# Layer B's x operands by token tile, its token sums taken in layer A's output projection, and its head norms' squares on ScalarE

## The chip, the cores and the metric

The kernel runs on one core of one Trainium2 chip. The metric is the device time of one execution in microseconds. A core has five engines with queues of their own: TensorE (PE; its weight loads are shown as PEld), VectorE (DVE), ScalarE (ACT), GpSimd (POOL) and SyncE (SP), which here issues the DMAs. Each engine works through its instructions in the order of the program and waits on semaphores for what others produce.

## The reference

Two attention layers run over 2048 prompt tokens and 64 sample tokens, `D_MODEL` = 1024, heads of 64, in float32. What is computed, cut to what matters here:

```python
def rms_norm(x, g):
    return x * rsqrt(mean(x * x, -1) + EPS) * g

def layer(x, norm_g, w_in, q_g, k_g, w_out, ...):
    h = rms_norm(x, norm_g)                      # one scale per token
    q, k, v, gate = split(h @ w_in)
    q, k = rms_norm(q, q_g), rms_norm(k, k_g)    # one scale per token and head
    o = softmax(q k^T / 8 + bias) v              # over a band of chunks of 64 tokens
    return x + (o * silu(gate)) @ w_out
```

Layer A has 16 query heads over 2 key heads and a window of 3 chunks, layer B has 16 heads with keys of their own and a window of 9 chunks. The kernel also returns the newest keys and values of both layers (for layer B the last 512 prompt tokens and the sample's).

## The kernel before

**Numbers as two parts.** A float32 product is made of three float32r products: x is split into `xh` (ScalarE's cast) and `xl` (GpSimd's subtraction x - xh), the weights into `wh` (ScalarE, times the norm's gain) and `wl` (VectorE), and PE adds `xh wh + xh wl + xl wh` (lines 481 to 483 in `project`). The sample's 64 tokens take two products, with the parts of x side by side in one stationary operand (474 to 477).

**Order of the work.** The tokens are cut into units of 256 (two tiles of 128), `u` = 0 to 7, and the sample, `u` = 8, which goes before unit 7. PE's order is written out by hand: `layer_a` and `layer_b` each have an attention pipeline, and in between its steps a `Filler` feeds the projections as jobs: layer A's input projections (four quarters `qd` of heads over all units), layer A's output projection (two halves of the outputs, eight jobs `j` of `OT` = 264 tokens each), layer B's input projections (eight head pairs `hp` over all units), layer B's output projection. When a job starts, `Filler.step` (622) runs the splits of its x and prefetches the x of the job after it; the weights of the third job ahead start with `WN - 8` = 5 pieces (640). The pipelines run the jobs as far as marks (`filler.to`, `PACE_B`) say. The instructions of the other engines are put in order by a planner that simulates the times; small tasks wait in the queue `bg` (`Background`) and are let in by `share` and `drain`, urgent ones first.

**x of layer B.** `load_act` (351) loads four pieces of a unit, each 256 inputs by all tokens of the unit, into `xraw`, a ring of `XB` = 3 buffers, and splits them into the ring `xx` of `XN` = 7 (lines 385, 386). For head pair 0 the split parts are also stored to `xsb` in DRAM (389); the other pairs load them from there (362). Each `xx` buffer is used by both token tiles of the unit, since a tile's projection runs over all eight blocks of 128 inputs.

**Token scales.** For layer B, `load_act` squares each piece on ScalarE into `res` (397) and adds it on VectorE into `sqr` (401, 403). `token_scales` (423) lets PE sum over the partitions with `ones` (430), VectorE takes mean and epsilon (`ms`, 433), and GpSimd the power of -1/2 (`rms`, 437). In layer B it is called in the first pair, after the first tile's products of each unit, with a result buffer of the ring `pj` of two, which the projections also use. In layer A, units 0 and 1 do likewise; for the others `row_scales` (444) loads the rows of x once more, four halves a unit, into the same ring `xraw` (454), and ScalarE squares and sums them (456).

**Behind a projection.** `evacuate` (490) empties `pj` on ScalarE with the token's scale (503). `head_norm` (511) takes each head's sum of squares on VectorE, one instruction a head (521), GpSimd the power (525), and VectorE scales (530). `gate` uses ScalarE's Tanh (538) into the ring `sq` of two, and `store_kv` (548) multiplies keys on GpSimd into `ko`, a single buffer (551), and stores them (552).

**Output projection.** `output_jobs` (1248) loads two blocks of the residual x into `res` (1275), PE makes 24 products for each of four blocks `m` of 128 outputs (1280 to 1282), VectorE adds (1285), and every second block is stored to `x1` (layer A) or `y` (1287).

Of the kernel before, what the change touches and what calls it, by code (L numbers as in the profile page):

```python
# [33 lines left out]
XB = 3  # L34
XN = 7
EARLY = 3
MORE = 4.7
WN = 13
# [13 lines left out]
def hybrid_encoder_kernel(  # L52
# [61 lines left out]
    mhalf = const([P, 4], "mhalf")  # L114
# [111 lines left out]
    xs = [dr.tile([P, 2 * KC * TOK], F32, tag=n, name=n) for n in ("xsa", "xsb")]  # L226
# [124 lines left out]
    def load_act(src, o, T, squares=False, joint=False, lead=None, cache=None, cached=False):  # L351
# [14 lines left out]
        def fetch():  # L366
            c = len(raws)
            if c < 4:
                raw = t("xraw", [P, 2 * OT], XB)
                rv = raw[:, : 2 * T].rearrange("p (k s) -> p k s", k=2)  # L370
                held["last"] = load(rv, src[:, 2 * c : 2 * c + 2, o : o + T]).ins
                raws.append(rv)
# [21 lines left out]
        def square(c):  # L394
            def fn():
# [4 lines left out]
                part = t("sqr", [P, 2 * T if joint else T], 2)  # L400
# [20 lines left out]
    rr = [const([P, NT + 1], f"rms{l}") for l in range(2)]  # L421

# [21 lines left out]
    def row_scales(unit):  # L444
# [4 lines left out]
        for i, (_, t0, n) in enumerate(tiles):  # L449
            r0 = (tt + i) * P  # L450
            for h in range(2):
                raw = t("xraw", [P, 2 * OT], XB)
# [11 lines left out]
        nc.gpsimd.tensor_tensor(rr[0][:, tt : tt + w], v[:, :w], mhalf[:, :w], op=ALU.pow)  # L464

# [24 lines left out]
    def evacuate(layer, tt, n, ps, C, G, b=None):  # L490
        a = t("pa", [P, 384], 4)
        pieces = [(a[:, : C - G], ps[:, : C - G])]
        if G:
            out = a
            if b is None:
                b = t("pb", [P, 256], 5)
# [14 lines left out]
    def head_norm(n, src):  # L511
        H = src.shape[1] // HD
        f = []

        def squares():
            sq = t("sq", [P, 256], 2)
            f.append(t("f", [P, 4], 3))
# [14 lines left out]
        return [bg.put(0.15 * H, squares, True), bg.put(0.1 * H, scale, True)]  # L532
# [79 lines left out]
    class Filler:  # L612
# [9 lines left out]
        def step(self):  # L622
            if self.gen is None:
# [13 lines left out]
                if self.n + EARLY < len(self.jobs):  # L637
                    nxt = self.jobs[self.n + EARLY]
                    if nxt.weights is not None and nxt.early:
                        nxt.weights(WN - 8)  # L640
# [17 lines left out]
    def layer_a():  # L658
# [4 lines left out]
        def add_unit(qd, place, unit):  # L663
# [8 lines left out]
            def prefetch():  # L672
# [3 lines left out]
                cache = None if qd < KEEP[u] else xs[0]  # L676
# [308 lines left out]
    def layer_b():  # L985
# [4 lines left out]
        def add_unit(hp, unit):  # L990
# [7 lines left out]
            def prefetch():  # L998
                for j in range(NO):
                    assert finished["x1", j] == 2 or j * OT >= u * UT + T  # L1000
                st.x[hp, u] = x = load_act(x1, u * UT, T, hp == 0, T == TS, None, xs[1], hp > 0)
                return x

            def weights(*m):
                if hp not in st.emit:
                    (st.w[hp],), _, st.emit[hp] = load_weights(1, (w_in_b[hp], 512))
                st.emit[hp](*m)

            def gen():
                xc = st.x.pop((hp, u))  # L1010
                it.prs, it.todo = [], []
                it.gate = t("pb", [P, 2, P], 5)
                for e, (tt, t0, n) in enumerate(tiles):
                    out = []
                    c = yield from project((tt, t0, n), xc, st.w[hp], 512, out)
                    if hp == 0 and e == 0:
                        token_scales(1, unit, xc, psum("pj", 512, 2))
                    pr = evacuate(1, tt, n, out[0], 512, P, it.gate[:, e])
                    it.prs.append(pr)
                    v, kn = pr[:n, 256:384], pr[:n, 128:256]  # L1020
                    split_v(n, v, VS[:, 2] if last else VT[:, tt])
# [400 lines left out]
```

## Time and profile before

| | |
|---|---|
| median of 3 runs | 2317.17 us (2315.77 to 2439.61) |
| profiled execution | 2318.61 us, span 2316.8 us, mean granted clock 0.996 |
| busy, share of the span | PE 98%, PEld 86%, DVE 67%, ACT 62%, POOL 37% |
| DMA | 379.37 MB, mean 164 GB/s |
| layer A's start (0 to 130 us) | PE busy 109.57 us |
| layer A's output projection (690 to 864.7 us) | PE busy 174.41 of 174.70 us |
| layer B's first head pair (864.7 to 1015 us) | PE busy 135.79 of 150.30 us |
| a later head pair (1452.2 to 1606.5 us) | PE busy 153.48 of 154.30 us |

How it is read: the page gives busy time by engine; the windows view gives it for stretches, with the granted clock of TensorE; the waits view says for whom an engine waited (engine, own buffer and line, then the releaser; total us, times, longest us); the lines view groups instructions (count, busy us, mean ns of one, idle before them). Matmuls are pipelined, so their mean durations overlap, and a busy PE need not be at its peak. A wait for several semaphores is put down to the one that came last.

### The profile page before, as it was taken

What the parts mean: (1) busy time and instruction counts of PE and PEld (TensorE: products, weight loads), DVE (VectorE), ACT (ScalarE), POOL (GpSimd) and SP (SyncE); (2) the same over time, 40 slices, a digit from 0 to 9 for tenths busy, and PEclk for the clock granted to TensorE, in tenths of its full rate; (3) what the DMA queues carried; (4) which work ended last, traced back from release to release, by engine and by line L of the source; (5) the groups of instructions that cost most, each with busy time, mean ns of one, the idle gap of its engine ahead of it and who ended that gap; (6) DMA issues with size and microseconds to landing.
All of it is one profiled execution on the core that took longest, in us unless ns stands there. A gap on an engine that the chain in (4) does not pass through costs nothing. (4 is left out here: it accounts for less than half of the span.)

```text
span 2316.8 us, 42427 instructions
## 1 busy us (share of the span) xinstructions
PE 2262.0 (98%) x13981; PEld 1987.5 (86%) x13981; DVE 1548.6 (67%) x5198; ACT 1427.1 (62%) x3628; POOL 855.9 (37%) x1235
## 2 busy tenths in 40 slices
PE   8899999999999999999999999999999999999999
PEld 6787888888889997878888888888888888889999
DVE  7679989888782227776766767767667677676211
ACT  6778877777773326765665666656656666566321
POOL 5554533333255445442222222322322223224443
PEclk9999999999999999999999999999999999999999
DMA  7846546754446766454454543544444435443665
GB/s 252 255 156 204 168 125 204 234 172 148 143 136 200 221 206 232 140 181 150 134 158 128 151 147 105 179 135 138 152 129 151 147 101 179 133 126 107 192 185 147
DMA packets 232126, 379.37 MB, mean 164 GB/s; under 512 B 24721, under 2 KB 163361, under 8 KB 231873
## 3 DMA queue, kind: packets, MB, share of 16 engines
q1 hardware_dynamic: 231904, 376.65, 52.8%
q8 instruction: 110, 1.80, 0.3%
q14 instruction: 112, 0.91, 0.1%
HBM read 296.13 MB, written 82.08 MB: 163 GB/s over the span
## 5 line engine op out<-in xcount | busy, mean ns | idle before, releaser
L481 PE MATMUL pj<-wh,xx 128*128 128x512 f32 (+1 forms) x1648 | 669.6, 406 | 17.1 <-ACT pb L503 7.2
L483 PE MATMUL pj<-wh,xx 128*128 128x512 f32 (+1 forms) x1648 | 639.4, 388 | 0.0
L482 PE MATMUL pj<-wl,xx 128*128 128x512 f32 (+1 forms) x1648 | 636.3, 386 | 0.0
L483 PEld LDWEIGHTS pj<-wh,xx 128*128 128x128 f32 x1648 | 311.3, 189 | 67.4
L481 PEld LDWEIGHTS pj<-wh,xx 128*128 128x128 f32 x1648 | 312.7, 190 | 58.7 <-ACT pb L503 8.4
L386 POOL TENSOR_TENSOR xx<-xraw,xx 128x528 fp32r<-128x528 f32 (+1 forms) x200 | 264.9, 1340 | 223.6 <-ACT xx L385 216.9
L482 PEld LDWEIGHTS pj<-wl,xx 128*128 128x128 f32 x1648 | 313.4, 190 | 37.9
L525 POOL TENSOR_TENSOR f<-f,mhalf 128x4 f32<-128x4 f32 (+3 forms) x221 | 228.1, 1032 | 221.9 <-DVE f L521 212.1
L1118 ACT ACTIVATE p<-p,nm 128x640 f32<-128x640 f32 (+5 forms) x272 | 204.3, 751 | 169.9 <-DVE nm L1114 167.8
L1280 PE MATMUL pj<-xx,wh 128*128 128x264 f32 x1024 | 293.3, 286 | 0.3 <-DVE res L1285 0.3
L1281 PE MATMUL pj<-xx,wh 128*128 128x264 f32 x1024 | 291.3, 284 | 0.0
L1282 PE MATMUL pj<-xx,wl 128*128 128x264 f32 x1024 | 289.8, 283 | 0.0
L1114 DVE CUSTOM_DVE_ANT_0 p<-sb,BT 128x640 f32<-128x640 f32 (+5 forms) x272 | 196.6, 723 | 114.9 <-PE sb L1108 111.5
L567 DVE TENSOR_TENSOR pl<-sb,ph 128x640 fp32r<-128x640 f32 (+5 forms) x272 | 194.5, 715 | 112.4 <-ACT ph L566 109.8
L385 ACT CAST xx<-xraw 128x528 fp32r<-128x528 f32 (+1 forms) x200 | 123.5, 626 | 217.7 <-PE pj L1282 119.2
L981 POOL TENSOR_TENSOR o<-gt,o 128x256 f32<-128x256 f32 (+2 forms) x140 | 107.1, 765 | 372.4 <-issue 150.8
L566 ACT CAST ph<-sb 128x640 fp32r<-128x640 f32 (+5 forms) x272 | 164.4, 604 | 118.9 <-PE sb L594 114.2
L1285 DVE TENSOR_TENSOR res<-pj,res 128x264 f32<-128x264 f32 x128 | 55.0, 431 | 248.3 <-PE pj L1282 237.3
L1280 PEld LDWEIGHTS pj<-xx,wh 128*128 128x128 f32 x1024 | 192.7, 188 | 1.0 <-DVE res L1285 0.5
L1281 PEld LDWEIGHTS pj<-xx,wh 128*128 128x128 f32 x1024 | 192.4, 188 | 0.2
L1282 PEld LDWEIGHTS pj<-xx,wl 128*128 128x128 f32 x1024 | 192.6, 188 | 0.0
L521 DVE CUSTOM_DVE_ANT_0 sq<-pa 128x64 f32<-128x64 f32 (+1 forms) x850 | 169.8, 252 | 23.3 <-ACT pa L503 21.2
(191 smaller groups left out, 4822.8 us busy)
## 6 DMA issues: line engine op xcount, KB each, us to landing
xx<-xsb SPq DMA_DIRECT2D x224, 512.0 KB, 4.3
xx<-xsa SPq DMA_DIRECT2D x88, 512.0 KB, 4.7
xraw<-oga SPq DMA_DIRECT2D x64, 264.0 KB, 3.4
xraw<-ogb SPq DMA_DIRECT2D x64, 264.0 KB, 3.3
xsa<-xx SPq DMA_DIRECT2D x32, 512.0 KB, 4.4
wraw<-in_w_in_b_dram SPq DMA_DIRECT2D x64, 256.0 KB, 3.5
xsb<-xx SPq DMA_DIRECT2D x32, 512.0 KB, 3.7
xraw<-in_x_dram SPq DMA_DIRECT2D x40, 256.0 KB, 4.1
```

Of the source, the lines that this page charges most:

```text
L386: nc.gpsimd.tensor_tensor(xl, rv, xh.bitcast(F32), op=ALU.subtract)
L481: nc.tensor.matmul(ps[:n, :C], xh, wh, start=k == 0, stop=False)
L482: nc.tensor.matmul(ps[:n, :C], xh, wl, start=False, stop=False)
L483: nc.tensor.matmul(ps[:n, :C], xl, wh, start=False, stop=k == KC - 1)
L521: nc.vector.tensor_tensor_reduce(out=sq[:n, c], in0=src[:, c], in1=src[:, c], op0=ALU.mult, op1=ALU.add, scale=1.0, scalar=HD * EPS, accum ...
L525: nc.gpsimd.tensor_tensor(fv, fv, mhalf[:n, :H], op=ALU.pow)
L567: b = nc.vector.tensor_tensor(dst_lo, src, dst_hi.bitcast(F32), op=ALU.subtract)
L1114: mi = nc.vector.tensor_tensor_reduce(out=p[:n, :nk], in0=S[:n, o : o + nk], in1=bias[:n, b0 : b0 + nk], op0=ALU.add, op1=ALU.min, scale=1 ...
L1118: ex = nc.scalar.activation(p[:n, :nk], p[:n, :nk], AF.Exp, scale=-1.0, bias=nmh, accum_out=it.sm[:n, 2 * i + h : 2 * i + h + 1],)
L1280: nc.tensor.matmul(ps[:, :OT], wh, oh, start=k == 0, stop=False)
L1281: nc.tensor.matmul(ps[:, :OT], wh, ol, start=False, stop=False)
L1282: nc.tensor.matmul(ps[:, :OT], wl, oh, start=False, stop=k == KC - 1)
```

## The change

- **x of layer B** is loaded by `load_b` as four operands a unit: one token tile (of two) by half of the inputs (`A11`, `A12` for the first tile, `A21`, `A22` for the second), kept in DRAM as `xo`, one slot an operand; the sample is one operand. `project_b` uses them tile by tile. The loads from `x1` go in runs of 128 tokens.
- **Token sums of layer B** are taken in layer A's output projection: `add_squares` squares the two finished blocks on ScalarE and adds them on VectorE to a sum per token, behind the next block's residual addition. `scales_of` makes the scales for tiles 0 to 11 ahead of unit 0's first products and for the rest ahead of unit 1's. The sums lie in the rings `ev` and `row` and in parts of the bias tile `BT`.
- **Head norms in layer B** use `squares_whole`: one Square on ScalarE for all heads of a tile, one `tensor_reduce` and one `tensor_scalar` on VectorE. Layer A keeps one instruction a head.
- **Buffers**: `xraw` 5 (was 3), weight parts 15 (13) with still 5 early pieces, `pb` 6 (5), `f` wider; `sqr` and `ko` are gone, the partial sums of layer A's first units go to `ev` and `ko` to the ring `sq`. The scratch for software-made DMA descriptors shrinks to 1024.
- The diff also adds `block_weights`, `product`, `gen_blocks`, `gen_sample` and, in `load_b`, `sums`, which form products of sums of blocks. They are used for head pairs from `PLAIN` on; `PLAIN` is 8 and the head pairs are 0 to 7.

```diff
+XR = 5
+PLAIN = 8
+S_FIRST = (6, 7)
-WN = 13
+WN = 15
+WP = 5
...
-    xs = [dr.tile([P, 2 * KC * TOK], F32, tag=n, name=n) for n in ("xsa", "xsb")]
+    xs = dr.tile([P, 2 * KC * TOK], F32, tag="xsa", name="xsa")
+    xo = dr.tile([P, 8 * NU + 1, 8 * P], F32, tag="xo", name="xo")
...
-                raw = t("xraw", [P, 2 * OT], XB)
+                raw = t("xraw", [P, 2 * OT], XR)
...
-                part = t("sqr", [P, 2 * T if joint else T], 2)
+                part = t("ev", [P, 256], 4)[:, : 2 * T if joint else T]
...
+    def add_squares(half, m, o, rv):
+        s2 = t("p", [P, 640], 3)[:, : 2 * OT].rearrange("p (k s) -> p k s", k=2)
+        nc.scalar.activation(s2, rv, AF.Square)
+
+        def fn():
+            if half or m == 3:
+                nc.vector.tensor_tensor(s2[:, 0], s2[:, 0], s2[:, 1], op=ALU.add)
+            cut = (o // UT + 1) * UT
+            for t0, t1 in ((o, cut), (cut, o + OT)):
+                a, b = (s2[:, k, t0 - o : t1 - o] for k in range(2))
+                acc = sums_of(t0, t1 - t0)
+                if half or m == 3:
+                    b = acc
+                nc.vector.tensor_tensor(acc, a, b, op=ALU.add)
...
+        return fn
+
+    def scales_of(t0, t1):
+        ps = psum("o", 512, 1)
+        w = t1 - t0
+        for i in range(w):
+            tok = (t0 + i) * P
+            nc.tensor.matmul(ps[:, 2 * i : 2 * i + 2], sums_of(tok, P), ones, start=True, stop=True)
+        v = t("f", [P, 16], 3)[:, :w]
+        nc.vector.tensor_scalar(
+            v, ps[:, : 2 * w].rearrange("p (i e) -> p i e", e=2)[:, :, 0], 1.0 / D, EPS, op0=ALU.mult, op1=ALU.add
+        )
+        nc.gpsimd.tensor_tensor(rr[1][:, t0:t1], v, mhalf[:, :w], op=ALU.pow)
...
+    def project_b(e, n, xc, w, res):
+        ps = psum("pj", 512, 2)
+        for k in range(KC):
+            wh, wl = weights_of(w, k)
...
+                xh, xl = (a[:, k % 4] for a in xc.op["A%d%d" % (e + 1, k // 4 + 1)])
+                nc.tensor.matmul(ps, xh, wh, start=k == 0, stop=False)
+                nc.tensor.matmul(ps, xh, wl, start=False, stop=False)
+                nc.tensor.matmul(ps, xl, wh, start=False, stop=k == KC - 1)
...
+    def load_b(unit, hp):
...
+        def cached(n, i):
+            xx = t("xx", [P, 4 * OT], XN, F32R)
+            held["last"] = load(xx[:, : 8 * P].bitcast(F32), xo[:, i]).ins
+            return xx
+
+        def split(xx, xh, xl, rv, i):
+            nc.scalar.copy(xh, rv)
+            nc.gpsimd.tensor_tensor(xl, rv, xh.bitcast(F32), op=ALU.subtract)
+            store(xo[:, i], xx[:, : 8 * P].bitcast(F32))
...
+        def raws():
+            for e in range(2):
+                for i in range(2):
+                    r = t("xraw", [P, 2 * OT], XR)[:, :512].rearrange("p (k s) -> p k s", k=4)
+                    held["last"] = load(r, x1[:, 4 * i : 4 * i + 4, u * UT + e * P : u * UT + e * P + P]).ins
+                    raw["A%d%d" % (e + 1, i + 1)] = r
...
+    def head_norm(n, src, whole=False):
...
+        def squares_whole():
+            sq = t("sq", [P, 256], 2)
+            f.append(t("f", [P, 16], 3)[:, :4])
+            fv = f[0][:n, :H]
+            nc.scalar.activation(sq[:n, : H * HD], src, AF.Square)
+            nc.vector.tensor_reduce(fv, sq[:n, : H * HD].rearrange("p (h d) -> p h d", d=HD), axis=AX.X, op=ALU.add)
+            nc.vector.tensor_scalar(fv, fv, HD * EPS, 1.0, op0=ALU.add, op1=ALU.mult)
+            nc.gpsimd.tensor_tensor(fv, fv, mhalf[:n, :H], op=ALU.pow)
...
-            ko = t("ko", [P, 2 * HD], 1)
+            ko = t("sq", [P, 256], 2)[:, : 2 * HD]
...
-                st.x[hp, u] = x = load_act(x1, u * UT, T, hp == 0, T == TS, None, xs[1], hp > 0)
+                st.x[hp, u] = x = load_b(unit, hp)
...
+                if hp == 0 and unit is order[0]:
+                    scales_of(0, 12)
+                if hp == 0 and unit is order[1]:
+                    scales_of(12, NT + 1)
...
-                    c = yield from project((tt, t0, n), xc, st.w[hp], 512, out)
-                    if hp == 0 and e == 0:
-                        token_scales(1, unit, xc, psum("pj", 512, 2))
-                    pr = evacuate(1, tt, n, out[0], 512, P, it.gate[:, e])
...
+                    c = yield from project_b(e, n, xc, st.w[hp], out)
+                    pr = evacuate(1, tt, n, out[0], 512, P, gt[:, e])
...
                     nc.vector.tensor_tensor(rv[:, m % 2], ps[:, :OT], rv[:, m % 2], op=ALU.add)
+                    if "sq" in held:
+                        held.pop("sq")()
                     if m % 2:
                         store(xout[:, c : c + 2, o : o + OT], rv)
+                        if layer == 0:
+                            held["sq"] = add_squares(half, m, o, rv)
+                            if half == 1 and j == NO - 1 and m == 3:
+                                held.pop("sq")()
...
-    nc = _bacc.Bacc("TRN2", target_bir_lowering=False, num_devices=1)
+    nc = _bacc.Bacc("TRN2", target_bir_lowering=False, num_devices=1, dynamic_dma_scratch_size=1024)
```

More of the change, by code (lines that the diff above doesn't have):

```diff
@@ L451, in row_scales @@
             for h in range(2):
[L452 removed]
+                raw = t("xraw", [P, 2 * OT], XR)
                 for d in range(0, P, n):
@@ new lines, in product @@
+    def product(ps, xc, parts, p, start):
+        xh, xl = xc.op[OPERAND[p]]
+        for k in range(4):
+            wh, wl = parts(PIECE[p], k)
+            nc.tensor.matmul(ps[:, :256], xh[:, k], wh, start=start and k == 0, stop=False, skip_group_check=not start)
+            nc.tensor.matmul(ps[:, :256], xh[:, k], wl, start=False, stop=False, skip_group_check=not start)
+            nc.tensor.matmul(ps[:, :256], xl[:, k], wh, start=False, stop=k == 3, skip_group_check=not start)
+            if k < 3:
+                yield 3 * 256 / 2400
@@ L530, in scale @@
             nc.vector.tensor_tensor(sv, sv, fv.unsqueeze(2).to_broadcast([n, H, HD]), op=ALU.mult)
-        return [bg.put(0.15 * H, squares, True), bg.put(0.1 * H, scale, True)]
+        return [bg.put(0.15 * H, squares_whole if whole else squares, True), bg.put(0.1 * H, scale, True)]
     def gate(n, g):
@@ L1005, in weights, with take_qk @@
                 if hp not in st.emit:
-                    (st.w[hp],), _, st.emit[hp] = load_weights(1, (w_in_b[hp], 512))
+                    if hp < PLAIN:
+                        (st.w[hp],), _, st.emit[hp] = load_weights(1, (w_in_b[hp], 512))
+                    else:
+                        st.w[hp], st.emit[hp] = block_weights(w_in_b[hp])
                 st.emit[hp](*m)
+            def take_qk(e, pr):
+                n = tiles[e][2]
+                it.prs[e] = pr
+                it.todo += head_norm(n, pr[:n, 0:256], True)
@@ L1032, in add_unit @@
+            if T < UT:
+                it.cost = 8 * 2 * 512 / 2400
+            else:
+                it.cost = (8 * 6 * 512 if hp < PLAIN else 7 * 12 * 256) / 2400
+            filler.total += it.cost
             it.mark = filler.total
-            filler.add(prefetch, weights if u == 0 else None, gen)
+            filler.add(prefetch, weights if u == 0 else None, gen if hp < PLAIN else gen_blocks if T == UT else gen_sample)
         for hp in range(8):
@@ L1046, in queries @@
             tp = psum("tp", 512, 1)
-            for pr, (tt, t0, n) in zip(it.prs, tiles):
+            for e, (tt, t0, n) in enumerate(tiles):
+                pr = it.prs[e]
                 for j in range(2):
@@ L1210, in pipeline @@
                 if x + 2 < len(its):
+                    if its[x + 2].hp >= PLAIN and len(heads) == 4:
+                        end = c0 + 0.875 * PACE_B * len(heads)
                     near = its[x + 2].mark
```

293 lines of the change are left out of this document (274 added, 19 removed).

## The prediction

> **What bounds the kernel now.** I read the page first.
>
> ```profile
> span 2316.8 us, 42427 instructions
> ## 1 busy us (share of the span) xinstructions
> PE 2262.0 (98%) x13981; PEld 1987.5 (86%) x13981; DVE 1548.6 (67%) x5198; ACT 1427.1 (62%) x3628; POOL 855.9 (37%) x1235
> ```
>
> TensorE (PE) is without work for 2316.8 - 2262.0 = 54.8 us in all. The change takes no matmul away and makes none shorter, so 54.8 us, and what a lowered clock costs on top, is all that it can win. Where is that idle time? The windows view by stage answers (busy time of each engine in each stretch; the columns behind POOL are the granted clock, the DMA share and GB/s):
>
> ```profile
> 0.00:130.00 130.00, 109.57 (x621) 92.45 (x622) 88.69 (x300) 91.84 (x238) 68.54 (x104) 0.97 0.79 245
> 690.00:864.70 174.70, 174.41 (x1426) 173.69 (x1427) 44.21 (x96) 53.68 (x96) 78.41 (x69) 1.00 0.70 206
> 864.70:1015.00 150.30, 135.79 (x728) 113.38 (x727) 119.45 (x359) 102.78 (x249) 80.48 (x90) 0.98 0.57 193
> 1452.20:1606.50 154.30, 153.48 (x907) 132.67 (x905) 108.39 (x369) 97.05 (x245) 43.62 (x72) 1.00 0.47 142
> 108.00:120.00 12.00, 9.47 (x52) 8.03 (x51) 8.15 (x23) 8.67 (x23) 7.87 (x10) 0.86 0.84 272
> 866.00:876.00 10.00, 7.95 (x29) 6.49 (x30) 4.03 (x7) 3.54 (x7) 5.24 (x5) 0.83 0.95 326
> 924.00:936.00 12.00, 10.30 (x49) 8.50 (x48) 8.76 (x34) 6.08 (x17) 5.23 (x7) 0.86 0.23 77
> 1009.00:1021.00 12.00, 8.48 (x44) 7.62 (x44) 8.49 (x27) 5.69 (x13) 3.75 (x6) 0.86 0.58 183
> ```
>
> The first row is layer A's start: 20.4 us idle. The second is layer A's output projection: 0.3 us idle, and VectorE (DVE) busy for only 44 of 175 us. The third is layer B's first head pair, where x is split and squared: 14.5 us idle, the thickest spot behind the start. The fourth is one of the later head pairs: 0.8 us of 154.3. The last four rows are short stretches behind the longest stalls; the clock drops there to 0.83 to 0.86, which costs 0.14 x 12 or 0.17 x 10 = 1.7 us each.
>
> Who ends PE's idle time in 864 to 1015 us (waits view: total, times, longest):
>
> ```profile
> PE pj L481 <- DVE ms L433: 6.1, 5, 3.5
> PE pj L481 <- ACT xx L385: 2.3, 1, 2.3
> PE sb L594 <- DVE nm L1114: 2.1, 3, 1.7
> PE sb L594 <- DVE pl L567: 1.4, 1, 1.4
> PE o L1185 <- DVE pl L567: 1.4, 2, 1.0
> PE sb L594 <- ACT sq L538: 0.7, 1, 0.7
> ```
>
> The first row is `token_scales`: its sums stand in a buffer of the two-deep ring `pj` until VectorE has read them, and the next projection waits for that buffer. In layer A's start (30 to 130 us), PE's longest entry and ScalarE's (ACT) two longest, the latter for 0 to 130 us, are:
>
> ```profile
> PE pj L481 <- ACT pb L503: 7.2, 5, 2.5
> ```
> ```profile
> ACT res L456 <- DMA xraw<-in_x_rows_dram: 17.2, 15, 3.0
> ACT xx L385 <- DMA xraw<-in_x_dram: 7.4, 8, 2.7
> ```
>
> ScalarE empties `pj` late because, in its own order, it stands before that for 17.2 + 7.4 = 24.6 us at loads into `xraw`, a ring of three through which each unit sends eight loads.
>
> **The change, part by part.** With `PLAIN = 8` every head pair (0 to 7) takes the plain path: `block_weights`, `gen_blocks`, `gen_sample` and the `sums` of `load_b` never run. PE gets the same matmuls in the same shapes, the sums' matmuls included. What runs differently is this.
>
> *Token sums.* Out of layer B's first pair go 36 Squares (9 units of 4), 36 + 27 adds, `ms` and its waits:
>
> ```profile
> L397 ACT ACTIVATE res<-xraw 128x512 f32<-128x512 f32 x40 | 25.1, 629 | 8.6 <-DVE sqr L401 5.8 <-DMA xraw<-x 1.8 <-DVE ms L433 0.8
> ```
> ```profile
> L401 DVE TENSOR_TENSOR sqr<-res 128x256 f32<-128x256 f32 x40 | 29.0, 726 | 18.7 <-ACT res L397 11.0 <-PE pj L430 6.8
> ```
>
> They come back as 32 Squares of 528 columns in the output projection (32 x 0.63 = 20 us, ACT from 54 to 74 of 175 us) and 88 adds; at the 0.42 us of L403 below, too much as half are short pieces, 37 us (DVE from 44 to 81 of 175). Those engines have the room: cost 0. If the cover failed, it would be by `res` coming free late behind the Square; the Square runs beside the store of the same tile, so I expect nothing. The new `scales_of` sits ahead of units 0 and 1 in PE's order, its sums are finished a job earlier, and it uses `o`, not `pj`. So the 6.1 us go (bounds 0, if the wait only changes its name, and 6.1).
>
> *`xraw` from three to five.* The 2.3 us stall at the border to layer B, by SyncE's issues and VectorE (timeline: start, length):
>
> ```profile
> 859.79 2.10 SPq L371 DMA_DIRECT2D xraw<-x  x2
> 861.94 0.46 SPq L1287 DMA_DIRECT2D x<-res  x1
> 863.75 0.37 SPq L1275 DMA_DIRECT2D res<-in_x_dram  x1
> ```
> ```profile
> 866.72 0.77 DVE L1285 TENSOR_TENSOR res<-pj,res 128x264 f32<-128x264 f32 x2 [1.21 <-DMA res<-in_x_dram]
> ```
>
> Loads of x for layer B hold SyncE's queue from 859.79 on, because the ring of three is full; the residual load behind them is issued at 863.75 only, and VectorE empties `pj` at 866.72. With five buffers and no Square holding them the loads go at once: the 2.3 us go. In layer A's start a row load now waits for the read three loads before it; with five, only for loads whose data the unit before has already used, so the 24.6 us of ACT should mostly go and of PE's 7.2 us I take 0.8, 5.8 us (bounds 0 and 7.2), with the 1.7 us of clock behind them.
>
> *DVE late in the first pair.* Of the rest (2.1 + 1.4 + 1.4 + 0.7, and 0.2 in a row not shown, 5.8 us) the timeline shows a cause:
>
> ```profile
> 903.17 0.42 DVE L403 TENSOR_TENSOR sqr<-sqr,sqr 128x256 f32<-128x256 f32 x1
> 903.69 1.33 DVE L401 TENSOR_TENSOR sqr<-res 128x256 f32<-128x256 f32 x1
> ```
> ```profile
> 903.37 1.37 POOL L386 TENSOR_TENSOR xx<-xraw,xx 128x512 fp32r<-128x512 f32 x1
> ```
>
> The add at 903.69 takes 1.33 us where the same shape took 0.42 just before: it ends (905.02) 0.3 us behind GpSimd's (POOL) subtraction (904.74). GpSimd's splits stay, the adds that they hold go; I take half, 2.9 us (bounds 0 and 5.8). [...]
>
> *Clock in the first pair.* The dips behind 864.7 and 1010 follow waits that go (2.3 and 3.5 us): 2 x 1.7 = 3.4 us. The dip at 924 to 936 I leave.
>
> *Norm squares in layer B.* Per 128-token tile, four products become one Square, one reduction and one small operation:
>
> ```profile
> L521 DVE CUSTOM_DVE_ANT_0 sq<-pa 128x64 f32<-128x64 f32 x64 | 11.5, 234 | 0.1
> L530 DVE TENSOR_TENSOR pa<-pa,f 128x256 f32<-128x256 f32 x17 | 8.1, 477 | 3.7 <-POOL f L525 3.5
> ```
> ```profile
> L538 ACT ACTIVATE sq<-pb 128x256 f32<-128x256 f32 x64 | 26.8, 418 | 1.2
> ```
> ```profile
> L433 DVE TENSOR_SCALAR ms<-pj x9: 147/154/156, 875.4 to 1013.9; 128x4 f32<-128x4 f32 x8, 128x2 f32<-128x2 f32 x1
> ```
>
> The products cost 11.5 / 16 = 0.72 us a tile (rows of one head pair, 1452 to 1606 us). A reduction over 256 columns is not in the trace; it reads one 256-wide input, so between half and the whole of L530, 0.24 to 0.48, I take 0.42 (L403 above). With 0.15 for the small one: 0.57, so DVE wins 0.15 x 17 = 2.6 us a pair, and ACT gets 17 x 0.42 = 7.1 us (97 to 104 of 154). Neither is the bound. What is late there now:
>
> ```profile
> PE sb L594 <- DVE nm L1114: 3.7, 6, 0.9
> PE o L1185 <- DVE pl L567: 1.2, 5, 0.2
> ```
>
> That is 4.9 us over seven pairs (1015 to 2080 us), where the next pair's weights are split just then. Two more weight buffers (`WN` 15) let two of the three late splits move ahead; the Square on ACT works against it. I take 0 (bounds -4.9 and the second rival).
>
> *Operands by tile and half.* Four loads of 512 KB a unit as before, but the first buffer is free after a quarter of the unit, not after 10 of 16 steps, and the sample's four loads become one. SyncE's longest wait is just this release:
>
> ```profile
> SPq L362 <- PE pj L483: 460.9, 192, 10.5
> ```
>
> PE never waits for these loads in the later pairs (rows above), so the shorter wait buys nothing there. In the first pair x comes in runs of 512 bytes in place of 1 KB; 32 loads, a job ahead of use: 0.
>
> *`ko` moves into the ring `sq`.* New wait: a Square or Tanh two allocations on must wait until the store of `ko` has landed, and ACT's whole queue (exponentials, `ph`, the emptying of `pj`) stands behind it.
>
> ```profile
> out_dram<-ko SPq DMA_DIRECT2D x33, 64.0 KB, 3.5
> ```
> ```profile
> 1464.91 0.46 POOL L551 TENSOR_TENSOR ko<-pa,kgr 128x128 f32<-128x128 f32 x1 [1.09 <-DVE sm L1125]
> ```
> ```profile
> 1469.50 0.31 ACT L538 ACTIVATE sq<-pb 64x128 f32<-64x128 f32 x1
> ```
>
> Product 0.46 and landing 3.5 make 4.0 us; the next user came 4.6 us after it began. So it fits, barely: cost 1 us (bounds 0 and the third rival).
>
> **Sum.** 6.1 + 2.3 + 2.9 = 11.3 and 3.4 of clock in the first pair, 5.8 + 1.7 = 7.5 at the start, less 1: 21.2 us. The profiled execution took 2318.6 us, 1.8 more than its span; 2318.6 - 21.2 = 2297.4. The median of the runs, 2317.17, lies 1.4 under the profiled one: **2296 us**.
>
> **Rivals.** *The waits only change their names* (the next late thing, the splits on ACT and POOL, takes their place): only the 6.1 us go, 2318.6 - 6.1 - 1.4 = 2311. For it: POOL's 80 of 150 us in the first pair stay, and ACT stood at two kinds of load at the start. Against: each wait has its own cause in the rows.
>
> *ScalarE becomes late in layer B.* 136 tiles x 0.42 = 57 us more on ACT; if half of each Square reaches PE, 28.5 us, and the gains stay: 2296 + 29 = 2325. Against: ACT is busy 97 of 154 us, and no wait of the later pairs in the rows above ends on it. [...]
>
> *The store of `ko` holds ScalarE* (slower). 40 stores in layer B (5 a pair, by the code: four tiles and the sample). If the planner puts the next users right behind, each is held up to 4.0 us; if half reaches PE, 40 x 2.0 = 80: 2296 + 80 = 2376. It makes the kernel slower from 21 / 40 = 0.5 us each, and by over 2% (46 us) from 67 / 40 = 1.7 us. For it: the margin of 0.6 us above. Against: the order of ACT is planned with that wait known.
>
> **Chances.** Forecast 0.73, names only 0.14, ScalarE late 0.07, `ko` 0.06. The forecast's own range: all bounds that favour it (6.1 + 2.3 + 5.8 + 5.0 + 7.2 + 1.7 + 4.9 = 33) give 2284, less 2 for stalls not counted, 2282; without the start's 7.5 and half of the DVE part, 2307. With the two middle rivals the range is 2282 to 2324. A change of 2%, 46 us, is about what a measurement of this kernel tells from none. To win that, nearly all of the 54.8 us must go: 0.02, from the forecast's share. Slower by over 2% is `ko`'s case, mostly: 0.05. The rest, 0.93, within.
>
> **What would show it.** Right: no wait on `ms` and none of 2 us at the border to layer B; the first pair's idle under 5 us with at most one clock dip; ScalarE's wait for `in_x_rows` under 8 us; PE's 0.8 us in a later pair unchanged, ACT there at 104 us. Wrong: a wait on `f`, `sq` or `pa` of PE in layer B, ACT idle before Square or Tanh with the store of `sq` as its releaser, or idle time on `res` in the output projection.

## The result, and the profile after

The changed kernel takes **2289.11 us** (median of 5 runs, 2288.97 to 2293.63) against 2317.17 us (5 runs beside it): a ratio of 0.9884, 95% interval 0.9869 to 0.99, so 23 to 30 us faster. Predicted were 2296 us and a range of 2282 to 2324. The page of the changed kernel begins:

```profile
span 2287.3 us, 41688 instructions
## 1 busy us (share of the span) xinstructions
PE 2250.9 (98%) x13981; PEld 1984.5 (87%) x13981; DVE 1539.7 (67%) x4400; ACT 1466.8 (64%) x3757; POOL 854.8 (37%) x1225
```

PE's idle time fell from 54.8 to 36.4 us, and its busy time by 11.1 us with the same 13981 matmuls, so the busy time held losses too, in part a lowered clock (0.996 before, 0.998 after on average). To see where the 29.5 us of span went, both traces are cut at the same matmuls of PE's order. The windows view of the changed kernel at those cuts (columns as in the prediction):

```profile
0.00:119.50 119.50, 107.51 (x622) 92.54 (x623) 91.74 (x306) 94.87 (x249) 72.63 (x108) 0.99 0.86 280
119.50:226.30 106.80, 103.47 (x618) 88.25 (x617) 90.76 (x326) 87.39 (x239) 54.43 (x86) 1.00 0.57 182
677.40:856.20 178.80, 176.34 (x1427) 175.23 (x1427) 94.50 (x172) 69.54 (x124) 83.55 (x70) 0.99 0.69 205
856.20:991.40 135.20, 131.13 (x729) 111.63 (x727) 90.29 (x206) 92.14 (x230) 74.16 (x85) 0.99 0.63 212
1426.50:1579.60 153.10, 152.86 (x905) 132.42 (x905) 103.52 (x266) 102.05 (x263) 43.57 (x72) 1.00 0.48 143
991.40:2047.50 1056.10, 1054.91 (x6240) 913.30 (x6241) 712.55 (x1826) 700.46 (x1804) 298.95 (x495) 1.00 0.48 143
2047.50:2287.30 239.80, 230.91 (x1847) 226.50 (x1845) 78.03 (x170) 81.11 (x163) 99.15 (x94) 1.00 0.51 150
```

| stage (us) | before | after | difference | forecast |
|---|---|---|---|---|
| layer A's start (to 240.0 in before) | 240.0 | 226.3 | -13.7 | -7.5 |
| rest of layer A | 450.0 | 451.1 | +1.1 | 0 |
| layer A's output projection | 174.7 | 178.8 | +4.1 | 0 |
| layer B's first pair | 150.3 | 135.2 | -15.1 | -14.7 |
| the seven later pairs | 1065.0 | 1056.1 | -8.9 | +1 |
| the end, with layer B's output projection | 236.8 | 239.8 | +3.0 | 0 |

The first pair came as forecast, the start gave twice as much, the later pairs gave what was forecast as nothing, and three stages got longer. PE's waits in the first pair and in the two stages that lost most (waits view: first pair; layer A's output projection; the end):

```profile
PE tp L850 <- DVE pa L786: 2.8, 1, 2.8
PE sb L850 <- DVE pl L823: 1.2, 1, 1.2
```
```profile
PE pj L1664 <- DVE res L1669: 2.5, 3, 1.8
```
```profile
PE sb L850 <- DVE nm L1496: 2.1, 1, 2.1
...
PE pj L1664 <- DVE res L1669: 0.9, 1, 0.9
```

The waits on `ms` and the border stall are gone. In their place stand one wait for a head norm (`pa`), waits for residual sums (`res`) and, near the end, one for the softmax (`nm`).

### The profile page after: what moved, and what is told of

Same layout as the page of the kernel before. It is cut to its first block, busy times and chain, and to the rows that moved or that the text cites. A ratio compares the mean times of both kernels' runs of the same rounds, so it can differ in the third digit from the quotient of the medians.

```text
span 2287.3 us, 41688 instructions
## 1 busy us (share of the span) xinstructions
PE 2250.9 (98%) x13981; PEld 1984.5 (87%) x13981; DVE 1539.7 (67%) x4400; ACT 1466.8 (64%) x3757; POOL 854.8 (37%) x1225
## 5 line engine op out<-in xcount | busy, mean ns | idle before, releaser
L529 PE MATMUL pj<-wh,xx 128*128 128x512 f32 x1024 | 421.9, 412 | 0.0
L531 PE MATMUL pj<-wh,xx 128*128 128x512 f32 x1024 | 403.6, 394 | 0.0
L530 PE MATMUL pj<-wl,xx 128*128 128x512 f32 x1024 | 402.8, 393 | 0.0
L391 POOL TENSOR_TENSOR xx<-xraw,xx 128x528 fp32r<-128x528 f32 (+1 forms) x168 | 225.1, 1362 | 196.6 <-ACT xx L390 187.1
L728 PE MATMUL pj<-wh,xx 128*128 128x512 f32 (+1 forms) x624 | 245.5, 393 | 1.7 <-ACT pb L750 1.2
L729 PE MATMUL pj<-wl,xx 128*128 128x512 f32 (+1 forms) x624 | 232.7, 373 | 2.3 <-DVE wl L320 2.3
L730 PE MATMUL pj<-wh,xx 128*128 128x512 f32 (+1 forms) x624 | 233.4, 374 | 0.0
L531 PEld LDWEIGHTS pj<-wh,xx 128*128 128x128 f32 x1024 | 192.6, 188 | 45.1 <-POOL xx L649 0.4
L530 PEld LDWEIGHTS pj<-wl,xx 128*128 128x128 f32 x1024 | 194.1, 190 | 23.1
L529 PEld LDWEIGHTS pj<-wh,xx 128*128 128x128 f32 x1024 | 193.5, 189 | 23.4
L769 POOL TENSOR_TENSOR f<-f,mhalf 128x4 f32<-128x4 f32 (+1 forms) x136 | 137.8, 1013 | 193.6 <-DVE f L768 178.0
```

The lines of the kernel that those rows point to most:

```text
L391: nc.gpsimd.tensor_tensor(xl, rv, xh.bitcast(F32), op=ALU.subtract)
L529: nc.tensor.matmul(ps, xh, wh, start=k == 0, stop=False)
L530: nc.tensor.matmul(ps, xh, wl, start=False, stop=False)
L531: nc.tensor.matmul(ps, xl, wh, start=False, stop=k == KC - 1)
L728: nc.tensor.matmul(ps[:n, :C], xh, wh, start=k == 0, stop=False)
L729: nc.tensor.matmul(ps[:n, :C], xh, wl, start=False, stop=False)
```

## The experiments

Twelve kernels ran. Their profiles, cut at the same matmuls (us; the last column is the median of the runs, for which the kernel before had 2317.12, 2315.59 and 2317.27 in the three sets; `a_oldops`, `a_wn13`, `a_res3` and `a_ko` belong to the second, `a_wn14`, `a_dvesplit`, `a_13n` and `b_xr_sums` to the third). Medians of different sets are compared by their ratios to the kernel before. A stage's time comes from one profiled execution, and a dip of the clock in it weighs: in the changed kernel the granted clock was 0.50 from 702.40 to 705.80 us, and 3.4 us at half the clock are 1.7 us.

| kernel | start | rest of A | output A | first pair | later pairs | end | span | median |
|---|---|---|---|---|---|---|---|---|
| before | 240.0 | 450.0 | 174.7 | 150.3 | 1065.0 | 236.8 | 2316.8 | 2317.17 |
| `b_wn` | 239.2 | 448.7 | 176.3 | 151.6 | 1066.0 | 239.2 | 2321.0 | 2316.51 |
| `b_xr` | 223.8 | 451.2 | 176.7 | 148.1 | 1064.9 | 236.8 | 2301.5 | 2301.58 |
| `b_sums` | 239.2 | 453.0 | 175.8 | 132.3 | 1063.0 | 236.7 | 2300.0 | 2301.44 |
| `b_xr_sums` | 225.0 | 453.2 | 177.3 | 133.0 | 1061.7 | 236.7 | 2286.9 | 2287.88 |
| after | 226.3 | 451.1 | 178.8 | 135.2 | 1056.1 | 239.8 | 2287.3 | 2289.11 |
| `a_oldnorm` | 227.2 | 450.4 | 179.0 | 132.1 | 1058.9 | 240.6 | 2288.2 | 2288.06 |
| `a_oldops` | 226.1 | 449.8 | 176.6 | 137.3 | 1058.8 | 240.5 | 2289.1 | 2291.64 |
| `a_dvesplit` | 225.3 | 449.4 | 178.3 | 130.5 | 1056.5 | 239.4 | 2279.4 | 2283.39 |
| `a_wn14` | 225.5 | 451.2 | 178.8 | 133.3 | 1056.5 | 237.2 | 2282.5 | 2284.1 |
| `a_wn13` | 225.9 | 452.5 | 174.9 | 130.9 | 1056.0 | 236.5 | 2276.7 | 2280.82 |
| `a_res3` | 223.8 | 453.2 | 177.6 | 131.1 | 1057.3 | 236.6 | 2279.6 | 2281.3 |
| `a_ko` | 223.6 | 452.5 | 178.3 | 131.1 | 1056.3 | 236.2 | 2278.0 | 2280.97 |
| `a_13n` | 225.7 | 452.7 | 177.9 | 131.4 | 1058.2 | 237.4 | 2283.3 | 2287.84 |

### `b_xr`: the kernel before, with `xraw` of five

`XR` is 5, at both places that load into `xraw`; the descriptor scratch shrinks as in the change, in all kernels below too.

```diff
-                raw = t("xraw", [P, 2 * OT], XB)
+                raw = t("xraw", [P, 2 * OT], XR)
```

> The kernel before with one part of the change: the ring xraw has five buffers in place of three (and the smaller DMA scratch, which makes the room). Theory: layer A's start was slow because ScalarE stood at loads held back by the ring. Then PE's 7.2 us of waits on the emptying of pj between 30 and 130 us go, ScalarE's wait for in_x_rows falls from 17.2 us to under 8, layer A is some 13 us shorter by the end of its unit loop as in the changed kernel, and the 2.3 us stall at the border to layer B goes; the waits on ms (6.1 us) stay. Time about 2300 us. Rival: the start's gain comes from another part (weight ring, ev ring) or from a new order of the planner; then the start keeps its 7.2 us and the time stays at 2313 to 2317.

Measured: 2301.58 us, ratio 0.9933 (0.9916 to 0.9949). The start shrinks by 16.2 us, more than twice the 7.5 forecast, and the other stages take 0.9 us more together. Of the 16.2 us, 12.5 are idle time of PE (25.6 before, 13.1 here). PE's waits in its first 130 us, and then in its first pair of layer B:

```profile
PE o L482 <- ACT wh L313: 5.8, 1, 5.8
PE o L431 <- DVE sqr L404: 3.0, 1, 3.0
...
PE pj L482 <- DVE ms L434: 5.7, 6, 3.0
PE sb L595 <- DVE nm L1115: 3.3, 4, 1.7
...
PE pj L482 <- ACT xx L386: 1.4, 1, 1.4
```

`PE pj <- ACT pb`, 7.2 us before, is gone altogether. The token sums' waits stay, and of the border stall 1.4 us.

### `b_sums`: the kernel before, with its token sums in layer A's output projection

```diff
-                    if hp == 0 and e == 0:
-                        token_scales(1, unit, xc, psum("pj", 512, 2))
+                if hp == 0 and unit is order[0]:
+                    scales_of(0, 12)
...
+                        if layer == 0:
+                            held["sq"] = add_squares(half, m, o, rv)
```

> The kernel before with layer B's token sums taken in layer A's output projection and no Squares in layer B's first pair; ring of three, x operands and head norms as before. Theory: the 6.1 us of waits on ms go and VectorE's lateness in the first pair falls; the first pair is 8 to 13 us shorter, the border stall of 2.3 us stays or shrinks (no Square holds xraw), and the output projection gets no waits: 2305 us. Rival: the sums make the residual addition late, and the output projection takes 4 to 5 us more as in the changed kernel: 2309 us.

Measured: 2301.44 us, ratio 0.9932 (0.9917 to 0.9946). The first pair falls from 150.3 to 132.3 us. All of PE's waits there:

```profile
PE sb L638 <- ACT sq L582: 0.8, 1, 0.8
PE tp L638 <- ACT pa L547: 0.5, 1, 0.5
```

The ring `xraw` is still three here, and yet the border stall is gone: without the Squares three buffers are enough. In layer A's output projection PE has no wait at all here (175.8 us, 1.1 more than before); but the jobs of that projection begin ahead of the cut, and there PE waits 1.5 us for a residual sum, which it doesn't before, in a stretch that is 3.0 us longer.

### `b_xr_sums`: both together

> The kernel before with the ring xraw of five and the token sums in layer A's output projection; everything else (operands, norms, the ring of weight splits, ko) as before. Theory (these two parts are the whole gain but for the later pairs): 2287 (2285 to 2290), no wait on ms, the first pair as in the changed kernel, later pairs as before at about 154.3 us. Rival (the operands by tile are needed in the first pair, since without them x's loads come late once the sums are gone): 2291 or more, with waits of TensorE on xx or of ScalarE on the loads of x in the first pair.

Measured: 2287.88 us, ratio 0.9873 (0.9854 to 0.9892): 29.4 us, where the two alone gave 15.5 and 15.7. This is all that the whole change gives. The operands, the norms, the ring of weight splits and `ko` together add nothing to it, though the stages are not the same: later pairs 5.6 us shorter in the changed kernel, the other stages 6.0 us longer. The next runs take that balance apart.

### `b_wn`: the kernel before, with 15 buffers for weight splits

```diff
-WN = 13
+WN = 15
-                        nxt.weights(WN - 8)
+                        nxt.weights(5)
```

> The kernel before with 15 weight buffers in place of 13, still 5 pieces early. Theory: the 0.8 us that PE loses at the end of each later head pair comes from the last three pieces of the next pair's weights, which must wait for buffers and are split just then; with two more buffers that wait goes and each later pair takes 1.2 us less, about 7 us in all: 2310 us. Rival: the gain of the later pairs comes from the head norms leaving VectorE; then the later pairs keep their 154.3 us and the time is 2317 within 2.

Measured: 2316.51 us, ratio 0.9999 (0.9988 to 1.0011). Alone, nothing, and the later pairs stay: the rival. (Its profiled execution, 2322.78 us, lay above its median; its stages weigh less.)

### `a_oldnorm` and `a_oldops`: the changed kernel without its norms, and without its operands

```diff
-                it.todo += head_norm(n, pr[:n, 0:256], True)
+                it.todo += head_norm(n, pr[:n, 0:256])
```
```diff
-                st.x[hp, u] = x = load_b(unit, hp)
+                st.x[hp, u] = x = load_act(x1, u * UT, T, False, T == TS, None, xs[1], hp > 0)
...
-                    c = yield from project_b(e, n, xc, st.w[hp], out)
+                    c = yield from project((tt, t0, n), xc, st.w[hp], 512, out)
```

> The changed kernel with the head norms of layer B as before: four products on VectorE a tile in place of one Square on ScalarE and one reduction. Theory: norms are off the path; VectorE is 1 to 3 us busier a head pair, ScalarE 6 to 7 us less, time 2289 within 2 us. Rival: the norms bring the later pairs' gain of 1.2 us each; then the time is about 2296 us and PE waits again for nm and pl at the end of each pair.

> All of the change except layer B's operands by token tile and half the inputs: x is loaded, split and cached in the old pieces, with the old loader, and the ring xraw of 5, the token sums, the ring of weight splits and the norms stay as in the changed kernel. Theory (the operands by tile, which leave SyncE's queue sooner, are what took about 1.2 us off each later pair of layer B): a later pair goes back to about 154.3 us and the time is 2295 (2293 to 2298). Rival 1 (the whole ring of weight splits together with the norms took it off): later pairs stay at about 153.1 us and the time is 2289 (2287 to 2291). Rival 2 (the operands also paid in the first pair): over 2298.

Measured: 2288.06 us (ratio 0.9875, 0.986 to 0.989) and 2291.64 us (0.9894, 0.9867 to 0.9921). Neither moves the total by more than the measurement tells. In the seven later pairs each is worth the same: 1058.9 - 1056.1 = 2.8 us for the norms, 1058.8 - 1056.1 = 2.7 us for the operands. Together 5.5, and `b_xr_sums`'s 1061.7 less 1056.1 is 5.6, so they add up. The six kernels that have both parts lie at 1056.0 to 1057.3 there, so 2.7 us stand out, if not by much. `a_oldops` also has the ring `pb` back at five buffers, which was not tried alone, so its 2.7 us are those of both. The norms give theirs back in the first pair, 135.2 against 132.1 us.

### `a_wn13` and `a_wn14`: the changed kernel with fewer buffers for weight splits

```diff
-WN = 15
+WN = 13
```

> The changed kernel with the ring of weight splits back at 13. Theory (the ring's size is worth nothing, as it was worth nothing alone): 2289 (2287 to 2291). Rival (with the x loads out of the way the two further buffers let the splits of the next pair go early, and that is the later pairs' gain): 2295 (2293 to 2297).

> The changed kernel with a ring of weight splits of 14 (it has 15; with 13 it took 2280.8). The ring's size also changes the order that the planner writes for VectorE, ScalarE, GpSimd and SyncE; PE's order stays. Theory (the order that comes out with 15 is an unlucky one, and the buffers as such are worth nothing): 14 gives a time that need not lie between the two, by the stalls of its own order; I expect 2279 to 2292 and a stall pattern of its own, above all near GpSimd's splits at the start of layer B. Rival (each buffer more lets splits run earlier and in the way of others): between the two, 2284 to 2286, with the waits on res and on the head norms half of those with 15.

Measured: 2280.82 us with 13 (ratio 0.9847, 0.9831 to 0.9863) and 2284.1 us with 14 (0.9851, 0.9826 to 0.9876). Neither expectation for 13 held: **the two more buffers cost about 8 us** and do not help the later pairs (1056.0 against 1056.1). With 13, three stages get shorter at once: output A by 3.9, the first pair by 4.3, the end by 3.3 us. In `a_res3` and `a_ko` below, which have 13 too, the first pair and the end come out alike (131.1 both; 236.6 and 236.2), but output A does not (177.6 and 178.3). The 3.9 us there are therefore not the ring's alone. `a_ko` has a dip of the clock at the start of that stage, behind a wait of 2.3 us for a residual sum:

```profile
676.50:679.90 3.40, 3.40 (x17) 3.40 (x18) 1.96 (x8) 1.74 (x7) 1.08 (x4) 0.50 0.40 119
```

`a_wn13` has the same wait, 2.3 us, and no dip. The first pair of `a_wn13`, by the windows view:

```profile
853.30:984.20 130.90, 130.90 (x729) 111.61 (x727) 87.05 (x205) 90.84 (x228) 74.32 (x84) 0.99 0.65 221
```

PE has no wait left there. The ring's size also changes the order that the planner writes: set side by side, PE's order is the same in both programs, while about 70 of VectorE's 4400 instructions stand elsewhere. What that does shows in layer A's output projection. VectorE's timeline there (start, length), with 15 buffers and then with 13:

```profile
699.54 1.82 DVE L313 TENSOR_TENSOR wl<-wraw,wh 128x512 fp32r<-128x512 f32 x2
701.29 0.42 DVE L1669 TENSOR_TENSOR res<-pj,res 128x264 f32<-128x264 f32 x1
```
```profile
700.09 0.69 DVE L313 TENSOR_TENSOR wl<-wraw,wh 128x512 fp32r<-128x512 f32 x1
700.70 0.78 DVE L1669 TENSOR_TENSOR res<-pj,res 128x264 f32<-128x264 f32 x2
```

With 15 buffers two weight splits stand ahead of the residual sum for which PE waits 1.8 us; with 13 it is one, and PE waits 0.2 us there (0.5 in `a_res3`, 0.9 in `a_ko`). With 14 the median lies between, as the rival had it, but by the ratios 14 can't be told from 13, and its waits are not half as long: it has the wait for a head norm nearly in full (2.4 us), and the end nearly as with 13 (237.2). At the end the pattern is plain. The five kernels with 15 buffers take 239.2 to 240.6 us there (`b_wn` among them), the nine others 236.2 to 237.4. Whether the buffers as such or the order that they bring decides in the other stages, these runs don't separate.

### `a_dvesplit`: the splits of the first pair on VectorE

```diff
             nc.scalar.copy(xh, rv)
-            nc.gpsimd.tensor_tensor(xl, rv, xh.bitcast(F32), op=ALU.subtract)
+            nc.vector.tensor_tensor(xl, rv, xh.bitcast(F32), op=ALU.subtract)
```

PE's wait of 2.8 us for `pa` in the changed kernel has this timeline on VectorE and GpSimd (start, length, then idle time before):

```profile
875.77 1.40 POOL L649 TENSOR_TENSOR xx<-xraw,xx 128x512 fp32r<-128x512 f32 x1
875.92 1.27 DVE L768 TENSOR_SCALAR f<-f 128x4 f32<-128x4 f32 x1
...
877.55 1.16 POOL L470 TENSOR_TENSOR rms<-f,mhalf 128x5 f32<-128x5 f32 x1
...
878.77 1.00 POOL L769 TENSOR_TENSOR f<-f,mhalf 128x4 f32<-128x4 f32 x1
879.75 1.25 POOL L649 TENSOR_TENSOR xx<-xraw,xx 128x512 fp32r<-128x512 f32 x1
879.80 1.48 DVE L786 TENSOR_TENSOR pa<-pa,f 128x256 f32<-128x256 f32 x1 [2.61 <-POOL f L769]
```

The norm's small operation L768 (4 columns) takes 1.27 us beside a split, the power L769 queues behind the token scales' power L470, and the scaling L786 takes 1.48 us beside the next split.

> The changed kernel (ring of 15) with the subtraction x - xh of layer B's first pair on VectorE in place of GpSimd. In the changed kernel TensorE's longest wait there, 2.8 us at 878, is for a head norm's scaling: GpSimd's power stands behind a split of 1.25 us and the scaling on VectorE runs beside another one in 1.48 us in place of 0.43. Theory (GpSimd's splits hold the norms): the first pair loses 3 to 4 us, no wait on pa of 2 us is left there, and the time is 2285 (2283 to 2287). Rival (33 splits of 0.67 us, 22 us more, make VectorE, busy for 100 of 150 us, the late engine): the first pair has new waits on VectorE and the time is 2290 to 2296.

Measured: 2283.39 us, ratio 0.9857 (0.9835 to 0.9879). The first pair takes 130.5 in place of 135.2 us and PE's only wait there is 0.2 us. The splits themselves (minimum, median, maximum in ns):

```profile
L649 DVE TENSOR_TENSOR xx<-xraw,xx x33: 676/685/1202, 840.9 to 973.7; 128x512 fp32r<-128x512 f32 x33
```

They take 0.68 us on VectorE where GpSimd took 1.30 in the median (1.25 to 1.72). VectorE is busy for only 6 us more in the whole execution (1545.7 against 1539.7) though it does 33 x 0.68 = 22 us more work: what it no longer loses beside GpSimd's splits makes up most of the rest (in the first pair its other work falls from 90.3 to 75.9 us). The norm's scaling there, in the changed kernel and then here:

```profile
L786 DVE TENSOR_TENSOR pa<-pa,f x15: 419/615/1511, 873.9 to 990.0; 128x256 f32<-128x256 f32 x14, 64x256 f32<-64x256 f32 x1
```
```profile
L786 DVE TENSOR_TENSOR pa<-pa,f x15: 393/419/615, 868.1 to 982.2; 128x256 f32<-128x256 f32 x14, 64x256 f32<-64x256 f32 x1
```

So GpSimd's splits do hold the norms. Whether PE waits for a held norm depends on the order as well: in `a_wn13` a scaling still takes 1.49 us beside a split (at 868.35), and PE has no wait in the first pair.

### `a_res3`: three buffers for the residual

The ring `res` gets three buffers at all six uses, and the ring of weight splits goes back to 13 for room.

```diff
-                        res = t("res", [P, 2 * OT], 2)
+                        res = t("res", [P, 2 * OT], 3)
```

> The changed kernel with the ring of weight splits at 13, which frees the room, and the ring res of three buffers in place of two. In the changed kernel layer A's output projection starts its later half 5.3 us late against the kernel before: TensorE waits 1.8 us twice for a residual sum and has one dip of the clock. Theory (a buffer of res comes free late, because ScalarE's Square now also reads it, so the next residual load lands late): the waits on res in layer A's output projection fall under 1 us in all and the time is 2284 (2282 to 2286), if the ring of 13 is worth nothing. Rival (the residual add itself is late on VectorE, behind weight splits and sum adds, whatever the buffers): the waits stay and the time is 2289 (2287 to 2291).

Measured: 2281.3 us, ratio 0.985 (0.9834 to 0.9865), the same as `a_wn13`'s 2280.82. PE's waits on `res` in the whole execution:

```profile
PE pj L1664 <- DVE res L1669: 3.6, 3, 2.3
```

They stay (2.6 us in `a_wn13`; within the stage's cut 1.3 against 0.3): the theory of the late buffer falls. VectorE is late with the sum, whatever the ring. The groups of VectorE in the changed kernel's output projection (count, busy us, mean ns) say with what:

```profile
L1669 DVE TENSOR_TENSOR res<-pj,res 128x264 f32<-128x264 f32 x57 | 24.3, 428 | 52.7 <-PE pj L1666 52.7
L447 DVE TENSOR_TENSOR p<-p 128x264 f32<-128x264 f32 x22 | 22.4, 1018 | 16.9 <-ACT p L443 16.9
L454 DVE TENSOR_TENSOR ev<-p,ev 128x248 f32<-128x248 f32 (+6 forms) x19 | 14.9, 815 | 0.4
...
L313 DVE TENSOR_TENSOR wl<-wraw,wh 128x512 fp32r<-128x512 f32 x8 | 6.5, 846 | 2.7 <-ACT wh L312 2.7
```

The new sum adds take 1.0 and 0.8 us on average, where the forecast put 0.42; the residual sum, with one input in PSUM, stays at 0.43 (all 57 between 0.42 and 0.44). That fits GpSimd's splits (L391), which run beside them: the add L447 at 781.35, with no split running, took 0.43 us, the one at 787.71, beside a split, 1.53. For this stage it wasn't tried.

### `a_ko` and `a_13n`: `ko` in its own buffer, and the old norms, both with the ring of 13

```diff
-            ko = t("sq", [P, 256], 2)[:, : 2 * HD]
+            ko = t("ko", [P, 2 * HD], 1)
```

> The changed kernel with ko in a buffer of its own, as before the change, and the ring of weight splits at 13 for room. Theory (the ko that shares the ring sq holds nobody): 2289 (2287 to 2291), no wait of ScalarE or GpSimd on a store of ko longer in the one than in the other. Rival (the products of VectorE or the Square of the norms wait for the store of ko now and then, which delays the heads): about 2 us less in layer B's pairs that hold the last four token tiles, 2284 to 2287.

> The changed kernel with the ring of weight splits at 13 and layer B's head norms as four products a tile, as before the change. Theory (the norms as such are worth about 0.6 us a later pair, the rest of what they seemed to cost was order): 2284 (2282 to 2287), later pairs 0.6 us longer than with the ring of 13 alone. Rival (the norms cost, as the comparison at 15 had it, 2288.1 against 2289.1): 2279 to 2281.

`a_ko`: 2280.97 us, ratio 0.9847 (0.9829 to 0.9865), as `a_wn13`; the expected 2289 was missed because of its ring of 13, not because of `ko`. In `a_ko` GpSimd waits 1.6 us, once, for the store of its own single buffer; in the changed kernel all that ScalarE waits for the store of `ko` is

```profile
ACT sq L794 <- DMA out_dram<-sq: 1.6, 1, 1.6
```

`a_13n` (norms as four products, ring of 13): 2287.84 us, ratio 0.9871 (0.9851 to 0.9891), above both expected ranges and by the ratios 5.6 us slower than `a_wn13`, so by these the norms pay once the ring is 13 (the two intervals overlap a little). Its later pairs take 1058.2 us, 2.2 more than `a_wn13`'s, and that is what can be put to the norms; another 3.0 us are in layer A's output projection (177.9), which the norms' code doesn't touch and which takes 177.6 and 178.3 us in the other two kernels with 13.

## Why the prediction was right or wrong, point by point

**Token sums and the first pair: right in the waits, in part by luck in the number.** Forecast 14.7 us, measured 15.1; `b_sums` shows 18.0 from the sums alone. No wait on `ms`, none at the border, 4.1 us idle (under 5), clock 0.99. Three readings inside it were off. The border stall was put down to the ring of three and the Squares together; `b_sums` removes it with the ring at three. Of VectorE's later waits the forecast took half, 2.9 of 5.8 us. Without the adds they vanish (`b_sums` has 1.3 us of waits in the whole pair, none on VectorE), but in the changed kernel new ones of 4.0 us come in, 2.8 of them the norm held by the splits. It is the wait on `pa` that the prediction named as a sign of being wrong. And the dips of the clock, 3.4 us in the sum, came out otherwise: the one at the border stayed (859.4 to 862.8 in the changed kernel, at 0.50) though its wait went, the one at 924 to 936, which the forecast left, went, and the one behind 1010 lies past the cut, in the later pairs. By the two parts, PE's idle time fell by 10.4 us where 11.3 were forecast, its busy time by 4.7 where 3.4 were.

**Layer A's start: right in its mechanism, mis-sized by half.** The step "of PE's 7.2 us I take 0.8, 5.8 us" counted only the waits whose releaser was ScalarE. With the ring of five alone, 16.2 us go: PE's waits on `pb` fall from 7.2 us to none, but its waits on VectorE in the whole stage also fall, from 11.7 to 7.3 us. That VectorE was late because its inputs come from ScalarE fits this, and wasn't followed row by row. The 1.7 us of clock are as forecast: of the dips at 31.7 and 113.7 us one is left. ScalarE's wait for `in_x_rows` in the first 130 us fell from 17.2 to 8.7 us, short of the "under 8":

```profile
ACT res L505 <- DMA xraw<-in_x_rows_dram: 8.7, 6, 3.5
```

**Output projection "cost 0": wrong, +4.1 us.** The step "Those engines have the room" failed: VectorE had room on average (94.5 of 178.8 us), but its order puts adds and weight splits ahead of the one sum that PE waits for. PE's idle time grew by 2.2 us (from 0.3 to 2.5), and a dip of the clock behind the wait of 1.8 us costs 1.7 more:

```profile
702.40:705.80 3.40, 3.40 (x17) 3.40 (x17) 2.65 (x4) 1.46 (x3) 3.40 (x4) 0.50 0.89 205
```

The adds were also too cheap in the forecast (VectorE 94.5 us where 81 was forecast). The 4.1 us are not the sums' alone: `b_sums` is 1.1 longer here without a wait, `b_xr` and `b_wn`, which have no sums, 2.0 and 1.6, `b_xr_sums` 2.6. How they share in the changed kernel stays open.

**Later pairs "I take 0": wrong, 8.9 us.** 3.3 us come with `b_xr_sums`, at the same idle time of PE (5.5 us in both). About half of them are a dip of the clock in the kernel before, behind its wait of 3.5 us on `ms` and just past the cut at 1015, which the forecast had counted in the first pair; the rest stays open:

```profile
1014.80:1018.20 3.40, 3.40 (x17) 3.20 (x16) 1.96 (x8) 2.55 (x8) 1.67 (x4) 0.50 0.11 31
```

The norms are worth 2.8 us (2.2 with the ring of 13) and the operands, with `pb`, 2.7. "PE never waits for these loads, so the shorter wait buys nothing" does not stand against `a_oldops`, if the ring `pb` is worth nothing, though by which path the operands pay is open: SyncE's longest wait for the release fell from 10.5 to 5.9 us in the changed kernel,

```profile
SPq L644 <- PE pj L531: 554.8, 186, 5.9
```

and is 10.8 again in `a_oldops`, but PE's waits there name VectorE's `pl` (3.0 us against 1.6), not x. The prices of the norms held in part: the reduction took 0.42 us as forecast, and ScalarE stands at 102 of 153 us where 104 were; but VectorE won 5.0 us a pair (747.5 us in `a_oldnorm` against 712.6, over seven pairs) where 2.6 were forecast. PE's idle time in a later pair did not stay at 0.8 us, it fell to 0.2.

**The ring of 15: wrong in sign.** The prediction let two more buffers help the late splits. They left the later pairs as they were and cost about 8 us elsewhere, most of it in the first pair and at the end.

**The rivals.** "The waits only change their names" (2311) falls by the first pair and the start. "ScalarE becomes late" falls: it got 33 us more in the later pairs (667.9 to 700.5), and they became shorter. With the Squares on ScalarE the later pairs, where PE waits for VectorE, are 2.8 us shorter (1056.1 against 1058.9 in `a_oldnorm`). The total doesn't show it with the ring of 15, and with the Squares' place the number of instructions changed too, so the place alone wasn't tried. "The store of `ko`" falls with `a_ko`: ScalarE did wait for that store, which the prediction had named as a sign of being wrong, but once, for 1.6 us, and the time is the same without it. Two small sums don't close: this ScalarE rival is priced at 2325 and the range ends at 2324, and 2296 without the start's 7.5 and half of VectorE's 2.9 us is 2305, not 2307.

The forecast of 2296 thus lies 7 us above the measurement as a sum of errors of both signs: 16 us more than forecast gained at the start and in the later pairs, 8 us lost in three stages where no loss was forecast.

**A better version.** The changed kernel with `WN = 13` takes 2280.82 us; its interval against the kernel before (0.9831 to 0.9863) lies wholly below the changed kernel's (0.9869 to 0.99).

## What to carry to other kernels

Time a change's parts alone and together: here two of six parts gave as much as the whole, and a harmless-looking one, two more buffers, took back what two good ones earned. When one engine is late, look in the waits view for the engines that it feeds: in `b_xr` PE's waits on VectorE fell from 11.7 to 7.3 us along with the 7.2 us on ScalarE, and the forecast, which counted only the waits in ScalarE's name, was too small. Where a planner writes the order, any new size is also a new order, so read a part's worth from a stage that repeats (seven pairs), not from the total.

## What the runs showed of the hardware that was not expected

A VectorE operation of four columns with one SBUF input took 1.27 us beside GpSimd's split (L768 above; 0.16 in the median), while a reduction over 256 columns beside such a split kept its 0.42 us:

```profile
871.01 1.28 POOL L649 TENSOR_TENSOR xx<-xraw,xx 128x512 fp32r<-128x512 f32 x1 [4.89 <-DMA res<-in_ckt_b_dram]
871.43 0.42 DVE L767 TENSOR_REDUCE f<-sq 128x4 f32<-128x256 f32 x1 [1.60 <-ACT sq L766]
```

From 860 to 1015 us all 18 reductions (L767) took 0.40 to 0.42 us. Why L768 is held and the reduction not, no run here shows. The prediction counted only the adds of the token sums as held by the splits, and so missed that the new norm brings a small operation which is held.

In `a_wn13` the clock fell to half for 3.4 us at the start of layer B with no wait of PE near it. PE's timeline and the windows:

```profile
853.40 1.84 PE L465 MATMUL o<-ones,ev 128*128 128x2 f32 x16
855.10 1.03 PE L465 MATMUL o<-ones,row 128*128 128x2 f32 x8
```
```profile
854.00:857.40 3.40, 3.40 (x26) 3.19 (x26) 1.51 (x3) 1.50 (x3) 3.40 (x4) 1.00 0.63 216
857.40:860.80 3.40, 3.40 (x9) 2.61 (x9) 2.17 (x6) 1.25 (x3) 2.45 (x2) 0.50 1.04 323
```

Just before it stand the 24 matmuls of two columns of `scales_of`, 2.6 us in which PE counts as busy. Eleven kernels have these matmuls. In the changed kernel such a dip begins at 859.40, 3.1 us after the first of them and again with no wait of PE near it; in `a_dvesplit` (853.4 to 863.6 us) and `b_sums` (866.8 to 873.6 us) the clock stands at 1.00 behind them. Over the whole first pair it is 0.99 in the changed kernel, `a_wn13`, `a_oldnorm`, `a_res3`, `a_13n` and `b_xr_sums`, 0.98 in `a_oldops`, and 1.00 in `b_sums`, `a_dvesplit` and `a_wn14`. That the matmuls cause the dip was not tried.
